# Layer 0's down projection as seven block products of 256 token columns, with its weight sums made earlier in the program

## The chip, the cores and the metric

One core of a Trainium2 chip runs the whole program in one launch. The metric is the device time of one execution in microseconds (us). Instructions go to five engines that run side by side, each strictly in its own order: TensorE (PE in the profile, its weight loads PEld), VectorE (DVE), ScalarE (ACT), GpSimd (POOL) and SyncE (SP). Transfers (DMA) are issued by SP, ACT or POOL and land later.

## The reference

Two layers of a decoder over 512 tokens, width 1024, feed-forward width 2816, all in float32:

```python
for l in range(DEPTH):                                     # DEPTH = 2
    p = rmsnorm(x, norm1_g[l]) @ w_in[l]
    p_rw, p_ret, p_sg, gate_logits = jnp.split(p, in_cuts, axis=-1)
    branches = jnp.stack([rwkv7_branch(p_rw, ...), retention_branch(p_ret, cos, sin),
                          sgu_branch(p_sg, ...)], axis=2)
    proj = jnp.einsum('bsgc,gcd->bsgd', branches, w_branch[l])
    gates = jax.nn.sigmoid(gate_logits.reshape(B, S, N_BRANCH, D_MODEL))
    x = x + jnp.sum(gates * proj, axis=2) @ w_out[l]
    x = x + conv_ffn(rmsnorm(x, norm2_g[l]), ffn_w_up[l], ffn_conv_w[l], ffn_conv_b[l], ffn_w_down[l])
return rmsnorm(x, final_g)
# conv_ffn: u = h @ w_up; causal depthwise convolution of width 3; (silu(gate) * val) @ w_down
```

## The kernel before

Activations lie with features on the 128 partitions and the 512 tokens in the free dimension. A float32 product is made of three matmuls (`mm3`): each operand is split into a high part (a cast, on ScalarE) and a low part (the rest, a subtraction on VectorE), and low x high, high x high and high x low are added in one accumulator. A weight unit is a 128x512 block (256 KB): `load` asks for it on SP's queue, `part` makes its high part (`sh` or `wh`, line 140) and low part (`sl` or `wl`, line 141), and `unit` keeps loads and splits a few units ahead of the matmuls (AHEAD). `acc` and `sm` are accumulators in PSUM.

A layer runs: the input projection with the recurrence (`rwkv`; eight chunks, whose steps on TensorE alternate with `fill`ed matmuls of other projections), then in `mixer` the branch outputs. There the string SEQ orders the pieces: S is a pair of retention chunks, Y (`ret_out`) normalises and transposes the retention output, and 0, 1 and 2 are the merges, the projections of the three branches times their gates. Around Y, VectorE makes `vt` (the gated retention rows, line 999) from `rrr`, a reciprocal root that GpSimd computes (line 996); TensorE transposes `vt` (line 1006); and each merge's accumulator is multiplied by its gate `gth` (line 1074), which was saved to memory (`gd`) earlier and is loaded back on GpSimd's queue (line 1071), then added by GpSimd (line 1077) or VectorE. After the mixer come the output projection (`wout`), the up projection (`ffn_up`, 22 chunks of gate and value columns, with the convolution and the activation `fth`) and the down projection.

Layer 0's down projection (`ffn_down`) takes 8 blocks of 128 output features; each adds 22 chunks of 128 inner features, three 512-column matmuls for each chunk: 528 matmuls. Layer 1's (`last`) is a seven-product block multiplication (Strassen's, in Winograd's form): the token half and the output half are split in two, sums of activations are the left operands (`halves` makes them in `ffn_up`), sums of weights the right ones. The weight sums are made beforehand by `presum`: per q (11 of them, 256 inner features each) four 128x512 loads `pre`<-`wdt` on GpSimd's queue, four VectorE passes (lines 251 to 254) and four stores `ts`; at the place where it is called next, the sums of the loads asked for at the call before are made. PRE says at which call the loads of q are asked for: during layer 0's up projection ("f") and after each output block of layer 0's down projection ("d").

A scheduler orders what the code hands it; instructions marked `kept` or `keep_in_program_order` stay where the code has them.

Of the kernel before, what the change touches and what calls it, by code (L numbers as in the profile page):

```python
# [26 lines left out]
PRE = {(0, "f", 2): 0, (0, "f", 4): 1, (0, "f", 6): 2, (0, "f", 8): 3, (0, "d", 0): 4, (0, "d", 1): 5, (0, "d", 2): 6, (0, "d", 3): 7,  # L27
       (0, "d", 4): 8, (0, "d", 5): 9, (0, "d", 6): 10}
SEQ = "0 H G G 0 S 0 U U G G 0 S 0 0 S 2 2 Y 0 0 2 1 2 1 2 1 2 1 2 1 2 1 1 1"
# [23 lines left out]
class Emit:  # L53
# [68 lines left out]
    def load(self, u, queue=None):  # L122
        name, l, i, c0, n, _ = u
        raw = self.u(n="wr") if u[5] in ("q", "u") and self.nraw % 2 else self.wp.tile([128, 512], F32, name=self.nm("wr"), tag="wr", bufs=NRAW)
        src = self.tsum[i] if name == "tsum" else self.a[name][l, i]
# [4 lines left out]

    def part(self, u):
        raw, n, pool = self.raws.pop(0), u[4], u[5]

# [112 lines left out]
    def presum(self, l, stage, m):  # L246

        if self.pre:
            q, b = self.pre.pop()
            V = self.nc.vector  # L250
            V.tensor_tensor(b[3], b[3], b[1], op=SUB)
            V.tensor_tensor(b[1], b[1], b[0], op=SUB)
            V.tensor_tensor(b[0], b[0], b[3], op=ADD)
            V.tensor_tensor(b[2], b[2], b[0], op=SUB)
            for p, t in zip((7, 5, 6, 4), (b[3], b[1], b[0], b[2])):
                self.tsum[q, p] = self.dp.tile([128, 512], F32, name=self.nm("ts"))
                self.nc.gpsimd.dma_start(self.tsum[q, p], t)
        q = PRE.get((l, stage, m))
        if q is not None:
            b = self.fpre.pop(0) if stage == "f" else [self.u(n="pre") for _ in range(4)]  # L260
            for i, t in enumerate(b):
                self.nc.gpsimd.dma_start(t, self.a["wdt"][0, 2 * q + i // 2][:, i % 2 * 512:i % 2 * 512 + 512])
            self.pre.append((q, b))

# [84 lines left out]
    def run(self):  # L349
        nc, tc, a, V = self.nc, self.tc, self.a, self.nc.vector  # L350
        self.con = self.cp.tile([128, NCC], F32, name="con")
        self.pre, self.tsum = [], {}
# [39 lines left out]
        for l in range(L):  # L392
# [7 lines left out]
            else:  # L400
                st = self.norm_new()
                x, xd = self.ffn_down(l, act, x, st)
# [8 lines left out]
    def mixer(self, l, nst):  # L411
# [27 lines left out]
        rows = iter([((), (0, 1), (0, 1, 2)), ((0, 1), (2, 3)), ((2, 3),)])  # L439
        for step in SEQ.split():  # L440
            if step == "S":
# [52 lines left out]
    def rwkv(self, l, nst):  # L494
# [210 lines left out]
        for c in range(8):  # L705
# [13 lines left out]
            V.tensor_copy(xb, Q[:, 1])  # L719
            self.fill(FILL[2], True)  # L720
# [18 lines left out]
            if c < 7:  # L739
# [3 lines left out]
                else:  # L743
                    V.tensor_tensor(St, St, Q[:, 0], op=ADD)
                    po(V.tensor_tensor(St, St, f, op=MUL))
            py = P1[:, 0]
# [735 lines left out]
```

## Time and profile before

| | |
|---|---|
| median of 3 runs | 1691.85 us (1691.11 to 1692.03) |
| span of the profiled execution | 1688.8 us (3.05 us below that median: what lies around the span) |
| granted TensorE clock | full in all 40 slices |
| busy: PE, DVE, ACT, POOL | 99%, 72%, 47%, 15% |
| layer 0: the merges behind the last retention matmuls, and the output projection | 398.9 to 505.5 |
| layer 0: up projection, down projection | 506 to 733.6, 733.6 to about 853 |
| layer 1: the same merges | from 1242.9 |

Times within a run count from the span's start. A row of the timeline is: start, duration, engine, line, operation, output<-input, shapes, count, and in brackets the idle time before it with what released it. The chain of waits follows the work that ended last backwards; its rows are start, duration, what. A row of the windows is: stretch, its length, busy time and count of the engine asked for (in the first such row below PE, in the later ones DVE), granted clock, share and rate of the DMA queues.

### The profile page before, as it was taken

Reading aid. Unit: us, or ns where it says so; the run is one execution under the profiler, and the core shown is the slowest. Engines: PE = TensorE matmul, PEld = TensorE weight load, DVE = VectorE, ACT = ScalarE, POOL = GpSimd, SP = SyncE. Lnnn points to the kernel's source line nnn. Section 1 sums busy time; section 2 is a strip of 40 time slices with the busy share of each in tenths; the row PEclk is TensorE's granted clock in tenths of the full one; section 3 lists DMA queues with packets and bytes.
Section 4 is the critical chain, followed back from the end, with each engine's and each line's share of the span. In section 5 each row is a group of like instructions: output and inputs, shape, how many; then the busy total and the mean of one; then the engine's idle time right before and its main releaser. Section 6 shows DMA issues by size and latency. Waiting matters only on the chain.

```text
span 1688.8 us, 27952 instructions
## 1 busy us (share of the span) xinstructions
PE 1680.2 (99%) x10247; PEld 1381.5 (82%) x10247; DVE 1217.9 (72%) x2115; ACT 793.7 (47%) x1365; POOL 261.3 (15%) x376
## 2 busy tenths in 40 slices
PE   9999999999999999999999999999999999999998
PEld 7888877888888888888888888778888888888887
DVE  7887746578669877655568888465786688887877
ACT  6563433554255444433346544335542544444565
POOL 1121000312301200003321210003122012220000
PEclk9999999999999999999999999999999999999999
DMA  5236563634544533247743366536344434443775
GB/s 183 88 109 199 176 187 95 184 122 134 191 144 148 195 122 97 63 146 261 252 145 99 94 207 184 174 101 188 118 137 163 154 96 144 142 141 110 244 248 177
DMA packets 143385, 260.01 MB, mean 154 GB/s; under 512 B 19440, under 2 KB 35440, under 8 KB 143248
## 3 DMA queue, kind: packets, MB, share of 16 engines
q1 hardware_dynamic: 117056, 188.41, 35.9%
q0 software_dynamic: 17552, 54.15, 9.8%
q10 hardware_dynamic: 8640, 15.67, 2.6%
q8 instruction: 80, 1.31, 0.3%
q14 instruction: 57, 0.47, 0.1%
HBM read 212.94 MB, written 45.22 MB: 153 GB/s over the span
## 4 chain that ended last, share of the span: by engine, by line
PE 97%; DVE 1%; DMA 1%; issue 0%; ACT 0%; SPq 0%; ACTq 0%; DVEq 0%
PE acc L157 88%; PE sm L157 3%; PE sm L696 2%; PE sm L948 1%; PE sm L603 1%; PE sm L1059 0%; DMA wr<-wall 0%; DMA tr<-bkT 0%; DVE wl L141 0%; PE acc L359 0%; PE sm L566 0%; PE sm L565 0%; PE sm L1006 0%; PE sm L850 0%; PE acc L319 0%
## 5 line engine op out<-in xcount | busy, mean ns | idle before, releaser
L157 PE MATMUL acc<-lo,sh 128*128 128x512 f32 x1108 | 432.0, 390 | 0.0
L157 PE MATMUL acc<-hi,sh 128*128 128x512 f32 x1108 | 431.4, 389 | 0.0
L157 PE MATMUL acc<-hi,sl 128*128 128x512 f32 x1108 | 424.6, 389 | 0.0
L140 ACT CAST sh<-wr 128x512 fp32r<-128x512 f32 (+1 forms) x375 | 226.8, 614 | 309.1 <-PE acc L157 165.6
L141 DVE TENSOR_TENSOR sl<-wr,sh 128x512 fp32r<-128x512 f32 (+1 forms) x375 | 252.0, 680 | 94.9 <-ACT sh L140 78.9
L141 DVE TENSOR_TENSOR wl<-wr,wh 128x512 fp32r<-128x512 f32 x238 | 169.0, 713 | 139.4 <-ACT wh L140 133.6
L140 ACT CAST wh<-wr 128x512 fp32r<-128x512 f32 x238 | 146.8, 619 | 242.8 <-PE acc L157 154.6
L157 PEld LDWEIGHTS acc<-lo,sh 128*128 128x128 f32 x1108 | 208.0, 188 | 43.8 <-issue 0.3
L157 PEld LDWEIGHTS acc<-hi,sl 128*128 128x128 f32 x1108 | 208.0, 188 | 43.1 <-issue 0.2
L157 PEld LDWEIGHTS acc<-hi,sh 128*128 128x128 f32 x1108 | 208.0, 188 | 43.0
L157 PE MATMUL acc<-lo,wh 128*128 128x512 f32 x584 | 230.0, 394 | 0.4 <-DVE rwp L525 0.4
L157 PE MATMUL acc<-hi,wl 128*128 128x512 f32 x584 | 228.3, 391 | 0.1
L157 PE MATMUL acc<-hi,wh 128*128 128x512 f32 x584 | 227.6, 390 | 0.0
L1125 ACT ACTIVATE cv<-fu,pc 128x512 f32<-128x512 f32 x88 | 71.7, 816 | 138.4 <-DVE fu L1123 138.4
L157 PEld LDWEIGHTS acc<-hi,wl 128*128 128x128 f32 x584 | 109.6, 188 | 24.6 <-issue 0.9
L157 PEld LDWEIGHTS acc<-lo,wh 128*128 128x128 f32 x584 | 109.6, 188 | 24.2 <-DVE rwp L525 0.8
L157 PEld LDWEIGHTS acc<-hi,wh 128*128 128x128 f32 x584 | 109.7, 188 | 22.3 <-issue 0.2
L157 PE MATMUL acc<-ah,sh 128*128 128x512 f32 x352 | 108.4, 389 | 0.0
L1126 DVE SCALAR_TENSOR_TENSOR cv<-fu,pc,cv 128x511 f32<-128x511 f32 x88 | 65.8, 749 | 34.5 <-ACT cv L1125 34.4
L157 PE MATMUL acc<-wl,hi 128*128 128x512 f32 x212 | 85.7, 404 | 0.0
L1123 DVE TENSOR_TENSOR fu<-acc,rsF 128x512 f32<-128x512 f32 x88 | 60.3, 685 | 30.8 <-PE acc L157 29.8
L157 PE MATMUL acc<-wh,hi 128*128 128x512 f32 x212 | 82.5, 389 | 0.0
(368 smaller groups left out, 2447.5 us busy)
## 6 DMA issues: line engine op xcount, KB each, us to landing
wr<-wall SPq DMA_DIRECT2D x480, 256.0 KB, 2.9
gd<-gth ACTq DMA_DIRECT2D x48, 256.0 KB, 3.4
gth<-gd POOLq DMA_DIRECT2D x48, 256.0 KB, 3.7
pre<-wdt POOLq DMA_DIRECT2D x44, 256.0 KB, 6.1
ts<-pre POOLq DMA_DIRECT2D x44, 256.0 KB, 2.8
wr<-ts SPq DMA_DIRECT2D x44, 256.0 KB, 4.1
wr<-wdn SPq DMA_DIRECT2D x40, 256.0 KB, 4.3
wr<-wdt SPq DMA_DIRECT2D x33, 256.0 KB, 4.1
```

Source lines behind the costliest of these rows:

```text
L140: self.kept(self.nc.scalar.copy(hi[:, :n], raw[:, :n]))
L141: self.kept(self.nc.vector.tensor_tensor(lo[:, :n], raw[:, :n], hi[:, :n], op=SUB))
L157: i = self.nc.tensor.matmul(*x, **y, **kw)
L603: i = T.matmul(pK[hv[1 - h], j, :], bk[hv[h], c, 1, :], x[hv[h], c, :], start=True, stop=True)
L696: po(T.matmul(o, l, r, start=start, stop=True, skip_group_check=True))
L948: po(T.matmul(o, lhsT, rhs, start=start, stop=stop, skip_group_check=True))
L1123: V.tensor_tensor(u, ps, self.rsF, op=MUL)
L1125: A.activation(t, u, AF.Identity, scale=self.p("cw2", j), bias=self.p("cb", j))
L1126: V.scalar_tensor_tensor(t[:, 1:], u[:, :511], self.p("cw1", j), t[:, 1:], op0=MUL, op1=ADD)
```

## The change

- Layer 0's down projection becomes `down`, the seven-product form with the operands' roles as follows: a weight block 128x128 stays in the array, 256 token columns move. Seven phases (products 1, 6, 2, 7, 5, 4, 3), each 11 units of q, each unit 4 output blocks x 3 matmuls of 128x256: 924 matmuls from 77 weight units (33 straight from `wdt`, 44 from the stored sums `ts`).
- `ffn_up` in layer 0 calls `halves` too; two of the four activation operands of a pair go to memory (`ab`, `s4`) and are read back and split in `down` (`side`).
- The 44 sums for layer 0 are new. Their places and those of layer 1's sums: two at a time in the recurrences (`rsum`, RSUM), at four "P" marks in SEQ among the merges (layer 0: q 3 to 6; layer 1: q 5, 7 and 9), in layer 0's up projection (layer 0's q 7 to 10), and in `down` at units 4 and 10 (layer 1's q 0 and 1), where `presum` is called after each of the first 22 units. For layer 1's q 4, 6 and 8 nothing is stored: the weights are loaded when `last` needs them and summed in place (NOW, `fetch4`, `sum4`).
- The residual and normalisation work of layer 0's end is done on 256-column halves as the products finish; the residual copy `xd` is stored in halves.

The core of the diff:

```diff
+PRE = {(0, "m", 0): (0, 3), (0, "m", 1): (0, 4), (0, "m", 2): (0, 5), (0, "m", 3): (0, 6),
...
+       (0, "d", 4): (1, 0), (0, "d", 10): (1, 1), (1, "m", 0): (1, 5), (1, "m", 1): (1, 7), (1, "m", 2): (1, 9)}
+RSUM = {(0, 0): (0, 0), (0, 2): (0, 1), (0, 4): (0, 2), (1, 0): (1, 2), (1, 2): (1, 3), (1, 4): (1, 10)}
+NOW = ((1, 4), (1, 6), (1, 8))
-SEQ = "0 H G G 0 S 0 U U G G 0 S 0 0 S 2 2 Y 0 0 2 1 2 1 2 1 2 1 2 1 2 1 1 1"
+SEQ = "0 H G G 0 S 0 U U G G 0 S 0 0 S 2 2 Y 0 P 0 2 P 1 2 1 P 2 1 2 P 1 2 1 P 2 1 1 1"
...
+    def sum4(self, b, p):
+        o, i, op = {7: (3, 1, SUB), 5: (1, 0, SUB), 6: (0, 3, ADD), 4: (2, 0, SUB)}[p]
+        return b[o], self.nc.vector.tensor_tensor(b[o], b[o], b[i], op=op)
...
+    def rsum(self, l, c, at):
+        if at and (l, c) in RSUM:
+            t = [self.rw((128, 2, 512), "cs", 3) for _ in range(2)]
+            q, b = RSUM[l, c], [t[i // 2][:, i % 2, :] for i in range(4)]
+            for i in range(4):
+                self.nc.gpsimd.dma_start(b[i], self.raw4(*q, i))
+            self.rs4 = q, b
+        elif (l, c - 2 + at) in RSUM:
+            q, b = self.rs4
+            for p in ((7, 5) if at else (6, 4)):
+                t, i = self.sum4(b, p)
+                self.tc.keep_in_program_order(i)
+                self.keep4(q, p, t)
...
-    def ffn_down(self, l, act, x, st):
-        for m in range(8):
-            ps = self.acc()
-            self.matF(ps, ("wdn", l, m, 0), act)
...
-            self.presum(l, "d", m)
+    def down(self, act, x, st):
...
+        for k, p in enumerate((1, 6, 2, 7, 5, 4, 3)):
...
+            for q in range(Q):
+                n = Q * k + q
+                w = self.unit("tsum", 0, (q, p), 0) if p > 3 else self.unit("wdt", 0, 2 * q + (p > 1), 512 * (p == 3))
+                side(n)
...
+                for j in range(4):
+                    ms, o = slice(128 * j, 128 * j + 128), ps[b][j // 2][:, 256 * (j % 2):256 * (j % 2) + 256]
+                    self.mm3(o, (w[0][:, ms], w[1][:, ms]), (xs[0][:, at:at + 256], xs[1][:, at:at + 256]), ...)
+                post(n)
+                if n < 22:
+                    self.presum(0, "d", n)
```

How the instructions stand after the change, at three places. The first is VectorE around the merges of layer 0. Before, the two `vt` groups of retention chunks 2 and 3 stand between gate passes (`gth`, L1074) and weight splits (`sl`):

```order
L1074 SCALAR_TENSOR_TENSOR gth_891_4552<-gth_891_4552,acc_892_4554 128x512
L994 TENSOR_SCALAR rss_889_4543<-rss_889_4543 128x4
L141 TENSOR_TENSOR sl_932_4707<-wr_920_4659,sh_931_4706 128x512
L999 SCALAR_TENSOR_TENSOR vt_681_3723<-ry_883_4524,rrr_887_4535,vt_681_3723 128x128 x4
L1074 SCALAR_TENSOR_TENSOR gth_896_4575<-gth_896_4575,acc_897_4577 128x512
L141 TENSOR_TENSOR sl_939_4734<-wr_925_4681,sh_938_4733 128x512
L999 SCALAR_TENSOR_TENSOR vt_683_3728<-ry_884_4527,rrr_890_4546,vt_683_3728 128x128 x4
L141 TENSOR_TENSOR sl_944_4757<-wr_930_4704,sh_943_4756 128x512
```

Now the second gate pass is `gth_914`; behind it come, in this order, one split, two sums (L153), a split, three sums, a split and three sums, and then these rows (the last of those sums at the top):

```order
L153 TENSOR_TENSOR pre_956_4777<-pre_956_4777,pre_954_4775 128x512
L169 TENSOR_TENSOR sl_994_4909<-wr_972_4836,sh_993_4908 128x512
L153 TENSOR_TENSOR pre_984_4875<-pre_984_4875,pre_982_4873 128x512
L153 TENSOR_TENSOR pre_982_4873<-pre_982_4873,pre_981_4872 128x512
L1045 SCALAR_TENSOR_TENSOR vt_699_3777<-ry_901_4578,rrr_905_4589,vt_699_3777 128x128 x4
L153 TENSOR_TENSOR pre_981_4872<-pre_981_4872,pre_984_4875 128x512
L1045 SCALAR_TENSOR_TENSOR vt_701_3782<-ry_902_4581,rrr_908_4600,vt_701_3782 128x128 x4
L153 TENSOR_TENSOR pre_983_4874<-pre_983_4874,pre_981_4872 128x512
L178 TENSOR_TENSOR lo_921_4658<-sm_919_4652,hi_920_4657 128x512
```

Eleven sums stand ahead of `vt_701`, the second group. The second place is GpSimd at the same stage. Before, it computes `rrr`, adds two gated merges and loads the next gates:

```order
L996 TENSOR_TENSOR rrr_870_4456<-rss_869_4453,con_78 128x4
L996 TENSOR_TENSOR rrr_887_4535<-rss_886_4532,con_78 128x4
L1077 TENSOR_TENSOR gth_790_4136<-gth_790_4136,gth_891_4552 128x512
L996 TENSOR_TENSOR rrr_890_4546<-rss_889_4543,con_78 128x4
L1077 TENSOR_TENSOR gth_810_4196<-gth_810_4196,gth_896_4575 128x512
L1071 DMA gth_913_4634<-gd_348_1650 128x512
```

Now fourteen `pre` loads stand between `rrr_888` and `rrr_905` (the last two of them are the first rows here), and the next gate load, `gth_931`, stands behind the stores of twelve sums (of which the last four are shown in the second fence):

```order
L284 DMA pre_1006_4965<-wdt 128x512
L284 DMA pre_1007_4966<-wdt 128x512
L1042 TENSOR_TENSOR rrr_905_4589<-rss_904_4586,con_78 128x4
L1042 TENSOR_TENSOR rrr_908_4600<-rss_907_4597,con_78 128x4
L1123 TENSOR_TENSOR gth_808_4190<-gth_808_4190,gth_909_4606 128x512
L1123 TENSOR_TENSOR gth_828_4250<-gth_828_4250,gth_914_4629 128x512
L284 DMA pre_1008_4967<-wdt 128x512
L289 DMA ts_950_4764<-pre_939_4713 128x512
```

```order
L289 DMA ts_1002_4954<-pre_984_4875 128x512
L289 DMA ts_1003_4957<-pre_982_4873 128x512
L289 DMA ts_1004_4960<-pre_981_4872 128x512
L284 DMA pre_1009_4968<-wdt 128x512
L289 DMA ts_1005_4963<-pre_983_4874 128x512
L1117 DMA gth_931_4688<-gd_348_1650 128x512
```

Layer 1 has the same order with twelve loads and ten sums. The third place is VectorE early in layer 0's down projection. Before, the sums of one q stand between the splits of that projection's units, one set per output block (66 matmuls):

```order
L141 TENSOR_TENSOR sl_1639_7745<-wr_1631_7706,sh_1638_7744 128x512
L251 TENSOR_TENSOR pre_1623_7664<-pre_1623_7664,pre_1621_7662 128x512
L252 TENSOR_TENSOR pre_1621_7662<-pre_1621_7662,pre_1620_7661 128x512
L253 TENSOR_TENSOR pre_1620_7661<-pre_1620_7661,pre_1623_7664 128x512
L141 TENSOR_TENSOR sl_1642_7763<-wr_1634_7724,sh_1641_7762 128x512
L254 TENSOR_TENSOR pre_1622_7663<-pre_1622_7663,pre_1620_7661 128x512
L141 TENSOR_TENSOR sl_1658_7806<-wr_1637_7742,sh_1657_7805 128x512
```

Now `sl_1717` and `sl_1724` are the splits of units 8 and 9, the four sums follow at once, and `wl_1731` is the split of unit 10; five units later the same happens ahead of unit 16's split:

```order
L169 TENSOR_TENSOR sl_1717_7908<-wr_1677_7773,sh_1716_7907 128x512
L169 TENSOR_TENSOR sl_1724_7934<-wr_1703_7833,sh_1723_7933 128x512
L153 TENSOR_TENSOR pre_1721_7926<-pre_1721_7926,pre_1719_7924 128x512
L153 TENSOR_TENSOR pre_1719_7924<-pre_1719_7924,pre_1718_7923 128x512
L153 TENSOR_TENSOR pre_1718_7923<-pre_1718_7923,pre_1721_7926 128x512
L153 TENSOR_TENSOR pre_1720_7925<-pre_1720_7925,pre_1718_7923 128x512
L169 TENSOR_TENSOR wl_1731_7964<-wr_1706_7851,wh_1730_7963 128x512
```

The four loads of that set stand on GpSimd directly behind the store of the last pair's `ab`.

More of the change, by code (lines that the diff above doesn't have):

```diff
@@ L249, in presum @@
             q, b = self.pre.pop()
[L250 to L257, printed above, removed]
+            for p in (7, 5, 6, 4):
+                self.keep4(q, p, self.sum4(b, p)[0])
         q = PRE.get((l, stage, m))
@@ L439, in mixer @@
         rows = iter([((), (0, 1), (0, 1, 2)), ((0, 1), (2, 3)), ((2, 3),)])
+        ip = iter(range(8))
         for step in SEQ.split():
-            if step == "S":
+            if step == "P":
+                self.presum(l, "m", next(ip))
+            elif step == "S":
                 self.ret_pair(*next(rows))
@@ L1187, in unit @@
             if p > 3:
-                return self.unit("tsum", 0, (q, p), 0)
-            return self.unit("wdt", 0, 2 * q + (p > 1), 512 * (p == 3))
+                return self.unit("tnow" if (1, q) in NOW else "tsum", 1, (q, p), 0)
+            return self.unit("wdt", 1, 2 * q + (p > 1), 512 * (p == 3))
         def prod(ps, x, at, r, w, first, end, **kw):
```

188 lines of the change are left out of this document (159 added, 29 removed).

## The prediction

> **What bounds the kernel now.** I read the page first (engines, clock, chain of waits), then the windows and the timeline of the stages that the diff touches.
>
> ```profile
> PE 1680.2 (99%) x10247; PEld 1381.5 (82%) x10247; DVE 1217.9 (72%) x2115; ACT 793.7 (47%) x1365; POOL 261.3 (15%) x376
> PEclk9999999999999999999999999999999999999999
> PE 97%; DVE 1%; DMA 1%; issue 0%; ACT 0%; SPq 0%; ACTq 0%; DVEq 0%
> 733.00:852.00 119.00, 119.00 (x527) 1.00 0.71 235
> ```
>
> TensorE is busy 99% at full clock and is 97% of the chain; layer 0's down projection (733 to 852) has no gap. So every matmul removed is time gained, and every wait newly put in front of TensorE is time lost. No cover is needed for what never makes it wait; vector work has 28% of the span free, but only where its order allows.
>
> **The gain: fewer matmul columns.** The chain's long unbroken piece prices a 512-column matmul, the kernel's last 36 accumulations a 256-column one (first and last row):
>
> ```profile
> 412.09 93.42 PE acc L157 x412
> 1678.60 0.28 PE L157 MATMUL acc<-sl,hi 128*128 128x256 f32 x1
> 1682.80 0.28 PE L157 MATMUL sm<-sh,lo 128*128 128x256 f32 x1
> ```
>
> 93.42/412 = 0.2268 us; 4.20/35 = 0.120 us, each with its own weight load. Before: 8 outputs x 22 chunks x 3 = 528 matmuls, 119.7 us. After: 7 x 11 x 4 x 3 = 924, 110.9 us. Gain 8.8 us. [...]
>
> **First loss: the sums at down's start.** `presum` is now called once per weight unit (12 matmuls x 0.120 = 1.44 us) instead of once per output column block (about 15 us). Loads asked for at unit 4 are summed at the next call, and on the vector engine those four sums stand ahead of the low half (`wl`) of unit 10. E is the moment the last up-projection matmul has issued, 733.38 + 0.23 = 733.6. Rows of the chain that leads to the loads, from layer 0 and from layer 1's same code, and then two rounds of presum:
>
> ```profile
> 733.38 0.39 PE L157 MATMUL acc<-hi,sl 128*128 128x512 f32 x1
> 737.09 0.69 DVE L1132 SCALAR_TENSOR_TENSOR fth<-fth,cv 128x512 f32<-128x512 f32 x1
> 1580.98 0.68 DVE L1132 SCALAR_TENSOR_TENSOR fth<-fth,cv 128x512 f32<-128x512 f32 x1
> 1581.77 0.43 DVE L1153 TENSOR_TENSOR wh<-fth,fth 128x256 f32<-128x256 f32 x1
> 1582.69 0.43 DVE L1155 TENSOR_TENSOR wl<-fth,wh 128x256 f32<-128x256 f32 x1
> 1583.03 1.28 DVE L141 TENSOR_TENSOR wl<-wr,wh 128x512 fp32r<-128x512 f32 x2
> 751.05 2.13 POOL L262 DMA_DIRECT2D pre<-wdt  x4
> 759.78 0.69 DVE L251 TENSOR_TENSOR pre<-pre,pre 128x512 f32<-128x512 f32 x1 [2.79 <-DMA pre<-wdt]
> 760.50 0.69 DVE L252 TENSOR_TENSOR pre<-pre,pre 128x512 f32<-128x512 f32 x1
> 763.42 0.54 POOL L257 DMA_DIRECT2D ts<-pre  x1 [0.66 <-DVE pre L254]
> 765.76 2.13 POOL L262 DMA_DIRECT2D pre<-wdt  x4
> 774.89 0.69 DVE L251 TENSOR_TENSOR pre<-pre,pre 128x512 f32<-128x512 f32 x1 [2.61 <-DMA pre<-wdt]
> gth<-gd POOLq DMA_DIRECT2D x48, 256.0 KB, 3.7
> ```
>
> The vector engine waits for these loads today (2.79 and 2.61 us), 8.7 and 9.1 us after the first issue; a unit of 2.7 us hides it. In the new order: the last gated activation starts at E+3.5; +0.8 to the half sums, +0.3 for the extra 256-column subtraction, +0.9, +0.3, two splits 1.2, the last half subtraction 0.4: E+7.5. Only then does GpSimd's store of `ab` issue (0.54), and behind it the four loads, from E+8.1. At 8.7 us the sums start at E+16.8, take 3 x 0.72 + 0.69 = 2.85, and unit 10's split 0.68: E+20.3. TensorE wants it at 10 x 1.44 + 0.24 = E+14.6. Stall 5.7 us. The second set (unit 10) is issued behind the first set's stores, E+20.5 (last sum + 0.84, the 763.42 row), so sums start at E+29.2 and unit 16's split is ready at E+32.7; TensorE, going on at E+20.3, is there after six units, E+28.9. Stall 3.8 us. Together 9.5.
>
> Bounds: if the last load lands 3.7 us after its issue (the gth row), first sum at E+13.9: 2.8 and 0.9, 3.7 in all; if it takes 12 us, because weights now come every 1.44 us instead of 2.72, 9 and 6, 15. I stay at 8.7, the same loads in the same stage. [...]
>
> **Second loss: the merges, both layers.** Rows of layer 0, then layer 1's, which are the same 844.0 us later:
>
> ```profile
> 398.92 5.67 PE acc L157 x24
> 404.58 0.22 PE sm L1006 x2
> 405.41 0.68 DVE L1074 SCALAR_TENSOR_TENSOR gth<-gth,acc 128x512 f32<-128x512 f32 x1
> 403.33 2.16 DVE L999 SCALAR_TENSOR_TENSOR vt<-ry,rrr,vt 128x128 f32<-128x128 f32 x4
> 406.61 2.17 DVE L999 SCALAR_TENSOR_TENSOR vt<-ry,rrr,vt 128x128 f32<-128x128 f32 x4
> 1239.68 1.13 DVE L999 SCALAR_TENSOR_TENSOR vt<-ry,rrr,vt 128x128 f32<-128x128 f32 x4
> 393.52 2.07 POOL L996 TENSOR_TENSOR rrr<-rss,con 128x4 f32<-128x4 f32 x2 [25.74 <-DVE rss L994]
> 403.27 1.28 POOL L1077 TENSOR_TENSOR gth<-gth,gth 128x512 f32<-128x512 f32 x1
> 407.79 2.19 POOL L1071 DMA_DIRECT2D gth<-gd  x4
> 410.67 1.42 PE sm L1006 x13
> 1242.91 5.67 PE acc L157 x24
> 1248.58 0.22 PE sm L1006 x2
> ```
>
> Today both `vt` groups are done at 408.8, before TensorE's transposes at 410.5, so nothing waits. In the new order eleven weight sums (ten in layer 1) and three weight splits stand with them ahead of the second `vt` group. The accumulator pass ahead of it can start when its 24 matmuls are done, about 404.8; then 0.6, one split 0.6, so the sums start at 406.0. Eleven sums at 0.60 (the x2 row: 1.28 - 0.68) to 0.72, say 0.66: 7.3; splits 1.8; two `vt` groups 2 x 1.05; and 1.03 twice, because a group beside GpSimd's addition takes 2.16 instead of 1.13 and two such additions move in here: done at 419.2. TensorE has 36 matmuls behind its first two transposes: 404.80 + 8.16 = 413.0. Stall 6.2 us. Then its next merge needs the fresh split: +0.5 (one cast, one subtraction, nothing else queued). The merge behind that needs an accumulator that is freed by a pass over `gth_931` (the name in the numbered order), whose load GpSimd issues only behind the stores of the twelve sums, about 420.5 instead of 407.8; it lands at 424.2, pass 0.7 us, 424.9; TensorE is there at 419.2 + 1.5 + 0.5 + 12 x 0.227 = 423.9, and a sum whose load is issued still later stands ahead of that pass: 2 us. Layer 0: 8.7; layer 1 with one sum less 8.0.
>
> Bounds, each layer: all loads in time, sums at 0.60, no stretch: stall 3.5, in all 4. Loads at the down stage's pace (four per 8.7 us; GpSimd asks for them from 395.6): the eleventh lands around 420, stall about 12, in all 14.5. I take 8.7: twelve loads and six of weights from 395.6 to 411 are 4.7 MB in 15.4 us, 306 GB/s, what a round of presum moves today:
>
> ```profile
> 766.00:775.00 9.00, 3.14 (x6) 1.00 0.90 300
> 600.00:643.60 43.60, 32.57 (x49) 1.00 0.31 99
> ```
>
> **Third loss: recurrences.** Two sums behind the state update and two behind the XB copy of chunks 1 to 6.
>
> ```profile
> 278.32 0.42 DVE L745 TENSOR_TENSOR S<-S,F 128x256 f32<-128x256 f32 x1
> 278.66 0.17 DVE s L756
> 281.00 0.42 DVE L719 COPY XB<-sm 128x256 f32<-128x256 f32 x1
> 282.57 1.09 PE sm L696 x64
> 283.25 0.69 DVE L141 TENSOR_TENSOR wl<-wr,wh 128x512 fp32r<-128x512 f32 x1 [1.04 <-ACT wh L140]
> ```
>
> At chunks 5 and 6 rotary work already fills the engine: XB is done 1.15 us before TensorE uses it, and two sums are 1.2 to 1.4 us; the next state update loses perhaps 0.9 more. Earlier chunks have idle time. 1.2 us a layer (0 to 1.5): 2.4.
>
> **Costed at nothing.** Layer 0's up projection: a pair of chunks (96 matmuls, 21.8 us) now takes six 256-column passes and one split where two splits stood, 6 x 0.43 + 0.68 - 1.36 = 1.9 more on 16.3 (half the last row's 32.57), and its sums stood there before: 18.2 of 21.8 covered; if that fails, 1 us. Down's 77 units at 0.6 us of splitting per 1.44 us; layer 1's sums in place likewise; its 24 saved transfers save nothing, since no wait stands there. The last phase's tail (about 5 us of vector work) is behind 36 column matmuls (8.2 us).
>
> **Sum.** -8.8 + 9.5 + 8.7 + 8.0 + 2.4 = +19.8 us. The profiled span is 1688.8, 3.05 below the median of 1691.85; the median moves by the same: 1711.7.
>
> **Rivals.**
> (a) Loads land quickly (3.7 us after issue, sums at 0.60): down loses 3.7, merges 4.5 and 4, recurrences 1.2: -8.8 + 13.4 = +4.6, 1696. For it: GpSimd's other loads do that. Against: the same loads' own 8.7 us.
> (b) Loads share the queues with the denser weights: down 15, merges 14 each, 2.4: +36.6, 1728. For it: eight or more loads at once, which the kernel before never has.
> (c) Faster: the cover holds in the merges. If the stretch from the `gth` pass to the second `vt` group takes under 8.2 us instead of 14.4 the vector engine keeps ahead of TensorE's 36 matmuls; then only down's stalls at their low bound stay, -8.8 + 3.7 + 1.2 = -3.9, 1688. It decides below 8.8 us of losses in all. Against: by the shortest rows that stretch is 11.7 us (pass and split 1.2, sums 6.6, splits 1.8, `vt` 2.1).
> (d) The block products give less than counted, e.g. because 77 units of weights at 182 GB/s plus operands reloaded from memory hold TensorE: the window above moves 235 GB/s, the round of presum 300. Part of (b).
>
> **Chances.** Forecast 0.62, (a) 0.18, (b) with (d) 0.13, (c) 0.04, and 0.03 that it lands within 0.2% (3.4 us, about what can be told from no change). Faster 0.04, same 0.04, slower 0.92. The range runs from (a) to just below (b): 1697 to 1727.
>
> **What would show it.** Around 405 to 425 and 844 + that: a gap of TensorE before the transposes, released by `vt`, and vector rows of `pre` in a block ahead of `vt`; a second gap released by a `gth` pass. Around 14 and 29 us after down's start gaps released by `wl`, with a vector wait on the `pre` loads before them. Down's matmuls at 0.120. Wrong if the merges show no gap, or if the `pre` loads are there before the vector engine asks.

## The result: 44 us slower, where 20 were forecast

The changed kernel takes 1735.96 us (median of 4 runs, 1733.88 to 1736.85), the kernel before beside it 1691.49: ratio 1.0261, 95% interval 1.0246 to 1.0275. The direction was right; the time lies 9 us above the range. The matmuls saved in layer 0's down projection gave what was forecast; the new weight sums, and the waits and slower clock that came with them, cost far more. The profiled execution of after has a span of 1732.2 us. Its page (engines, chain) and the cores' row:

```profile
PE 1687.8 (97%) x10643; PEld 1402.3 (81%) x10643; DVE 1297.4 (75%) x2287; ACT 819.3 (47%) x1436; POOL 311.4 (18%) x470
PE 74%; issue 12%; DVE 6%; DMA 4%; POOL 2%; ACT 1%; ACTq 0%; DVEq 0%; SPq 0%; POOLq 0%
core 0: 1732.2 us, clock 0.991
```

TensorE is 74% of the chain, 97% before: in some places the chain of waits now runs through transfers and vector work. And the clock is 0.991: it was full in every slice before. What TensorE waited for (total us, times, longest):

```profile
PE sm L1052 <- DVE vt L1045: 11.4, 4, 5.0
PE acc L185 <- DVE wl L169: 8.4, 5, 4.3
PE acc L185 <- DVE gth L1120: 5.7, 2, 3.9
PE sm L740 <- DVE S L790: 2.8, 4, 1.2
PE sm L740 <- DVE XB L763: 2.1, 1, 2.1
```

The first three are the waits that the prediction named: `vt` and a `gth` pass in the merges, `wl` in down. The next two are the recurrences; the last one is the first step of layer 1's. The table cuts both traces at the same marks of TensorE (first matmul of a stage to the first of the next; in the kernel before, 17 matmuls of 0.227 us that stand ahead of the up projection are counted to it, as in after). The mark at layer 1's recurrence stands behind the gap in its first step, so the row before it holds that gap. The last three columns belong to experiments 9, 10 and 17 below.

| stage, us | before | after | difference | form alone | form, early loads | cheapest places |
|---|---|---|---|---|---|---|
| layer 0, to the end of the recurrence | 289.1 | 290.7 | +1.7 | 289.3 | 289.1 | 292.8 |
| merges and output projection 0 | 97.1 | 111.2 | +14.1 | 97.8 | 97.4 | 98.1 |
| up projection 0 | 231.7 | 231.7 | 0 | 231.7 | 231.7 | 234.2 |
| down projection 0 | 119.7 | 122.0 | +2.3 | 111.0 | 110.9 | 116.5 |
| layer 1, norm to recurrence | 205.8 | 213.3 | +7.5 | 211.3 | 207.6 | 206.6 |
| recurrence 1 | 67.8 | 69.2 | +1.4 | 70.2 | 68.9 | 73.6 |
| merges and output projection 1 | 101.6 | 111.9 | +10.3 | 101.6 | 101.6 | 101.6 |
| up projection 1 and last phase | 332.8 | 337.9 | +5.1 | 333.9 | 334.3 | 334.7 |

The differences make 42.4 of the 43.4 us between the spans.

**The merges.** The chain through layer 0's merges (start, us, what):

```profile
399.57 6.24 DMA pre<-wdt
...
407.43 6.69 DMA pre<-wdt
...
414.15 0.68 DVE pre L153
...
421.06 1.05 DVE vt L1045 x4
...
423.01 0.53 POOL ts L289
423.54 4.43 DMA gth<-gd
...
430.51 0.69 DVE gth L1120
...
DMA to landing us min/median/max: 6.4/6.4/6.5
```

Two loads of `pre` in a row, a block of sums, `vt`; then the store of a sum, the gate load queued behind it, its pass. The last row is the answer for the four gate loads issued from 423.5 to 425.5: they took 6.4 us to land, so the first was there at 429.9, and not at 427.97, where its row of the chain ends. Three sums (428.45 to 430.6) stood ahead of its pass as well. TensorE's gaps, start to start: 5.41 and 1.65 us before `vt`'s transposes, 0.57, and 4.25 before the matmul behind that gate pass; in layer 1 3.57, 2.38, 0.58 and 2.19. Less the ordinary spacing they make 11.1 and 7.9 us. In layer 1 the last gap has another cause: the first gate load had landed at 1296.3, but its pass (1297.7) stood behind a weight split that waited for TensorE's own matmuls.

**Down.** The chain, then the first wait's row, then rows behind it:

```profile
757.83 0.52 POOL pre L284
...
770.37 7.87 DMA pre<-wdt
...
778.26 0.70 DVE pre L153
...
781.05 0.69 DVE wl L169
768.60 0.39 PE L185 MATMUL acc<-ah,wl 128*128 128x256 f32 x1 [4.32 <-DVE wl L169]
...
770.02 0.42 PE L185 MATMUL acc<-ah,wl 128*128 128x256 f32 x1
770.24 0.63 PE L185 MATMUL acc<-ah,wh 128*128 128x256 f32 x2
770.66 0.41 PE L185 MATMUL acc<-ah,wl 128*128 128x256 f32 x1
...
823.62 15.84 PE sm L185 x132
```

Once the sums are through, a matmul takes what was costed: 15.84/132 = 0.120 us (last row). The gaps are 764.00 to 768.60 and 778.71 to 781.79. But behind the first gap, from 770.02 to 770.66, three matmuls take 0.64 us instead of 0.36.

**The clock.** Windows of after (stretch, length, TensorE busy and count, granted clock, DMA share, GB/s): the six stretches at half clock in which TensorE has work, then one behind a gap of 2.34 us in layer 1's recurrence, at full clock; below, the merges of layer 0 before and after (each engine's busy time, then the clock):

```profile
418.00:424.80 6.80, 3.90 (x16) 0.51 1.02 382
431.70:435.10 3.40, 3.40 (x10) 0.52 0.57 219
769.60:773.00 3.40, 3.40 (x18) 0.52 0.88 240
783.20:786.60 3.40, 3.40 (x18) 0.51 0.96 302
906.10:909.50 3.40, 3.40 (x10) 0.51 0.43 151
1288.40:1295.20 6.80, 5.54 (x20) 0.51 0.83 295
...
1084.90:1088.30 3.40, 3.40 (x72) 1.00 0.72 223
```

```profile
395.00:440.00 45.00, 45.00 (x226) 37.60 (x225) 33.22 (x58) 15.86 (x29) 16.38 (x20) 1.00 0.49 158
395.00:440.00 45.00, 34.94 (x164) 28.55 (x163) 35.18 (x65) 11.76 (x22) 29.33 (x45) 0.89 0.79 281
```

Each stretch is 3.41 us or twice that and lies behind a gap of 3.1 us or more, or behind a cluster of gaps (902 to 906). TensorE is busy in 23.0 of their 27.2 us, so they cost at most 11.5. In down it is 3.0 (16 matmuls in each of two stretches, at 0.213 instead of 0.120 us); what the gaps leave over of the merges' loss is 3.0 of 14.1 and 2.4 of 10.3; with 1.6 at layer 1's start that is about 10 us of TensorE's time. It is not what a full clock would have saved: no run changed the clock alone, and where the next wait ends with a load, as behind the first stretch in down, a faster TensorE would only have waited longer.

The length of a gap alone does not decide: the longest of that cluster is 1.64 us, the one that full clock follows 2.34. In after's record of the granted clock the changes between full and half all lie on one grid of 3.413 us (the stretches between them last 3.413, 6.827, 10.24 us and so on), and half clock went with how long TensorE had worked within the window of that grid ahead. The window of after ahead of the stretch at 906; then, of experiment 12, one with a gap of 2.40 us and the half clock behind it; last, of experiment 7, the first of two windows that share a gap of 3.35 us, with no half clock behind either:

```profile
902.58:905.99 3.41, 1.59 (x7) 1.00 0.21 77
881.93:885.34 3.41, 1.40 (x7) 1.00 0.23 77
885.34:888.75 3.41, 3.41 (x10) 0.50 0.60 210
1116.91:1120.32 3.41, 1.79 (x8) 1.00 1.00 277
```

After's trace has 496 full-clock windows on that grid. All six in which TensorE was busy for less than 45% (0.24 to 1.32 us) were followed by half clock; of three between 46 and 49% one was (that at 902.58), and of the 487 above 58% none.

### The profile page after: what moved, and what is told of

Read it like the earlier page. It is cut to its first block, busy times and chain, and to the rows that moved or that the text cites. A ratio compares the mean times of both kernels' runs of the same rounds, so it can differ in the third digit from the quotient of the medians.

```text
span 1732.2 us, 29278 instructions
## 1 busy us (share of the span) xinstructions
PE 1687.8 (97%) x10643; PEld 1402.3 (81%) x10643; DVE 1297.4 (75%) x2287; ACT 819.3 (47%) x1436; POOL 311.4 (18%) x470
## 4 chain that ended last, share of the span: by engine, by line
PE 74%; issue 12%; DVE 6%; DMA 4%; POOL 2%; ACT 1%; ACTq 0%; DVEq 0%; SPq 0%; POOLq 0%
PE acc L185 66%; PE sm L185 4%; PE sm L740 2%; DMA pre<-wdt 2%; DVE wl L169 1%; DVE sl L169 1%; DVE pre L153 1%; PE sm L647 1%; DMA wr<-wall 1%; PE sm L994 0%; ACT wh L168 0%; PE sm L1105 0%; DMA wr<-ts 0%; POOL pre L284 0%; POOL ts L289 0%
## 5 line engine op out<-in xcount | busy, mean ns | idle before, releaser
L185 PE MATMUL acc<-lo,sh 128*128 128x512 f32 (+1 forms) x1144 | 444.9, 389 | 6.2 <-DVE gth L1120 5.7
L185 PE MATMUL acc<-hi,sh 128*128 128x512 f32 (+1 forms) x1144 | 443.8, 388 | 0.0
L185 PE MATMUL acc<-hi,sl 128*128 128x512 f32 (+1 forms) x1144 | 431.1, 388 | 0.0
L168 ACT CAST sh<-wr 128x512 fp32r<-128x512 f32 x352 | 212.0, 615 | 183.6 <-PE acc L185 83.7
L169 DVE TENSOR_TENSOR wl<-wr,wh 128x512 fp32r<-128x512 f32 x278 | 194.7, 706 | 136.0 <-ACT wh L168 131.8
L169 DVE TENSOR_TENSOR sl<-wr,sh 128x512 fp32r<-128x512 f32 x352 | 239.0, 692 | 68.7 <-ACT sh L168 60.2
L185 PE MATMUL acc<-lo,wh 128*128 128x512 f32 (+1 forms) x636 | 245.0, 385 | 0.0
L185 PE MATMUL acc<-hi,wl 128*128 128x512 f32 (+1 forms) x636 | 243.3, 382 | 0.8 <-DVE wl L169 0.8
L185 PE MATMUL acc<-hi,wh 128*128 128x512 f32 (+1 forms) x636 | 242.5, 381 | 0.0
L185 PEld LDWEIGHTS acc<-hi,wl 128*128 128x128 f32 x636 | 119.7, 188 | 25.4 <-DVE wl L169 1.8
L185 PEld LDWEIGHTS acc<-lo,wh 128*128 128x128 f32 x636 | 119.7, 188 | 23.8 <-DVE rwp L569 0.4
L185 PEld LDWEIGHTS acc<-hi,wh 128*128 128x128 f32 x636 | 119.7, 188 | 22.1 <-issue 0.2
L185 PE MATMUL acc<-wh,lo 128*128 128x512 f32 x212 | 82.5, 389 | 0.0
```

The costliest lines, as they stand in the source:

```text
L168: self.kept(self.nc.scalar.copy(hi[:, :n], raw[:, :n]))
L169: self.kept(self.nc.vector.tensor_tensor(lo[:, :n], raw[:, :n], hi[:, :n], op=SUB))
L185: i = self.nc.tensor.matmul(*x, **y, **kw)
```

## The experiments

The ratios are to the kernel before, run beside each (1690.3 to 1691.4 us); stage times are from each run's trace. Layer numbers in the edits count from 0.

**1. Down's sums spaced out.** `presum` is called at three units only:

```diff
-                if n < 22:
+                if n in (4, 10, 16):
```

> The changed kernel with the weight sums in layer 0's down projection asked for at units 4 and 10 and summed at units 10 and 16 instead of 5 and 11. Theory (sums whose loads have not landed hold up the splits behind them): both gaps of TensorE in that stage (4.6 and 3.1 us) go, and with them the two stretches of half clock behind them (about 3.3 us): 10 to 11 us less than the changed kernel, about 1725. Rival (the stage is short of transfer bandwidth with 77 weight units): the gaps move to a later unit and the time stays within 3 us.

1723.1 us, ratio 1.019 (1.0161 to 1.022). Down falls from 122.0 to 111.8 us; `wl`'s waits:

```profile
PE acc L185 <- DVE wl L169: 1.8, 3, 1.0
```

Both gaps and their half-clock stretches are gone: the same eight sums cost 0.9 us when six units instead of one lie between loads and sums. Their order, not their number, made down's loss.

**2. Layer 0's merges cleared.** Its four sets go to the up projection:

```diff
-PRE = {(0, "m", 0): (0, 3), (0, "m", 1): (0, 4), (0, "m", 2): (0, 5), (0, "m", 3): (0, 6),
+       (0, "f", 10): (0, 3), (0, "f", 12): (0, 4), (0, "f", 14): (0, 5), (0, "f", 16): (0, 6),
```

> The changed kernel with layer 0's four sets of weight sums taken out of its merges and made in layer 0's up projection (chunks 10 to 16) instead. Theory (the sums among the merges cost 14 us in that layer, the up projection covers them): about 14 us less, 1722, and no gap of TensorE around 405 to 435. Rival (the vector engine is too full in the up projection, or what is late in the merges is not the sums): gaps appear between 600 and 700, or the gap before the transposes stays; less than 5 us gained.

1726.2 us, 1.0209 (1.0179 to 1.0238). The stage returns to 97.1 us (-14.1), the up projection pays 1.2. So this price is the merges' own. The time falls by 10 only, since other stages of that execution were longer.

**3. No vector passes in the merges,** loads and stores kept (`keep4` gets the loaded tile):

> The changed kernel with the vector passes of the weight sums left out in the merges of both layers; their loads and stores stay as they are (the stores write unsummed weights, so the result is another one). Theory (eleven and ten vector passes stand ahead of the second vt group): the gaps before the transposes (5.4 + 1.7 and 3.6 + 2.4 us) mostly go; the later gap by a gate pass (4.3 and 2.2) may stay, since its load is still behind the stores; 10 to 16 us less in all. Rival (GpSimd's queue is the cause: fourteen loads stand ahead of the reciprocal roots): the gaps before the transposes stay above 3 us; at most 6 us less.

1732.3 us, 1.0245 (1.0187 to 1.0302). `vt`'s gaps shrink from 5.41 and 1.65 to 2.15 and 1.05, but the gate gap grows from 4.25 to 7.14: the stages gain 1.7 and 2.2 us only. The chain there:

```profile
414.82 1.60 POOL ts L289 x3
416.42 5.39 DMA ts<-pre
...
423.66 5.75 DMA gth<-gd
...
429.44 0.70 DVE gth L1120
```

GpSimd's stores and loads, in order, take the place of the vector engine.

**4. The gate loads on SP's queue** (`nc.sync.dma_start` at line 1117):

> The changed kernel with the gate loads of the merges asked for on SP's queue instead of GpSimd's, where they stand behind the weight sums' loads and stores. Theory A (in the merges two things are late one behind the other: the vector block ahead of vt, and the gate load behind the stores): the gaps before the transposes stay (about 5 to 7 us in layer 0, 5 to 6 in layer 1), the gaps released by a gate pass (4.3 and 2.2) go; 6 to 10 us less with the half clock behind them. Theory B (it is the transfers' landing, whatever queue): the gate gaps stay within 1 us of what they were.

1745.0 us, 1.0319 (1.0299 to 1.034). The gate gaps vanish and others come (2.42, 0.81 and 3.17 us later in layer 0's merges); the stage grows to 117.3. This is no way round the queue.

**5. The loads alone in the merges,** passes and stores left out:

```diff
+            if stage != "m" and q in ((0, 3), (0, 4), (0, 5), (0, 6), (1, 5), (1, 7), (1, 9)):
+                return
...
-                self.keep4(q, p, self.sum4(b, p)[0])
+                if stage != "m":
+                    self.keep4(q, p, self.sum4(b, p)[0])
```

> The changed kernel with vector passes and stores of the weight sums left out in the merges of both layers, their loads kept (unsummed weights are used in their place, so the result is another one). Theory (in the merges GpSimd's queue is the second limit: the gate load stands behind stores that wait for the loads): with the stores gone the gate gaps (7.1 and 3.6 us without the passes) shrink below 2 us, the stages lose 8 us or more each against the changed kernel. Rival (the loads alone fill the transfer queues): the gate gaps stay above 4 and 2 us.

1715.5 us, 1.0149 (1.0128 to 1.0169). The merges lose 3.3 and 3.0 us instead of 14.1 and 10.3, without gate gaps. So three limits stand one behind the other: passes ahead of `vt`, stores ahead of the gates, and some 3 us of the loads.

**6. No passes in the last phase's in-place sums:**

> The changed kernel with the in-place weight sums of layer 1's down projection left out (the unsummed weights are split and used instead). Theory (twelve passes more on a vector engine whose splits TensorE waits for there): the six gaps of 0.7 to 0.8 us around 1641 to 1705 go and the stage from layer 1's second norm to the end loses 4 to 5 us. Rival (the 24 direct loads, or their buffers, hold it up): under 1.5 us.

1735.0 us, 1.026 (1.024 to 1.0281), no gain, because other stages of that execution were longer; but the stage falls from 337.9 to 333.9, and the gaps of 0.72 to 0.80 us at 1641 to 1666 are gone. About 4 of its 5.1 us are these sums.

**7. No passes in the recurrences,** loads and stores kept:

> The changed kernel with the vector passes of the weight sums left out in both recurrences, loads and stores kept (the stores write unsummed weights). Theory (two passes behind the state update and two behind the XB copy): the gaps of 1.57 us at chunks 5 and 6 of both layers go; 2 to 3 us less. Rival (the loads disturb the transfers that the recurrence itself waits for): the gaps of 1.6 and 2.3 us in its first chunks stay, and so does most of the loss.

1745.2 us, 1.0321 (1.0291 to 1.035). The 1.57-us gap at chunk 6 is gone; new ones (3.51 and 3.35 us the longest) stand where the chain goes through a transfer:

```profile
208.26 4.69 DMA bkS<-tr
...
219.26 1.98 PE sm L738 x62
```

Here the loads can disturb more than the passes; how much varies between executions (1741.1 and 1749.2 us).

**8. The two `wua` loads of layer 1 ahead of both casts:**

> The changed kernel with the two small weight loads at the start of each layer (wua, on ScalarE's queue) both issued ahead of the casts that read them. Theory (at layer 1's start ScalarE stands 2.2 us at a load issued just ahead of its reader, which delays the norm factor and piles up work until TensorE waits at 888 and 903 to 907): the stage from the norm to the recurrence loses 4 to 5 us of its 7.5, about 1731. Rival (the pile-up is from the vector engine's halves at the end of down, or from late weight loads): under 1.5 us.

1738.4 us, 1.028 (1.0251 to 1.031). ScalarE's wait shrinks from 2.18 to 0.41 us, the gap at 888 is gone, one of 2.44 at 906 takes its place. Moved by a few instructions only, the loads gain nothing that shows.

**9. The form alone,** no weight sum in either layer (products use unsummed blocks):

> The seven-product form in both layers with every weight sum left out (no loads, passes or stores for them; unsummed weight blocks of the same size are used where sums stood, so the result is another one). Theory (the form gains 8.8 us by its matmuls and all the loss is the sums' and their places'): down takes 111 to 112 us against 119.7, the merges and recurrences are as before, 1683 to 1686. Rival (the form costs by itself at layer 1's start, where its tail of halves comes late): the stage behind layer 1's first norm stays 3 to 5 us longer than before, 1687 to 1690.

1688.3 us, 0.9993 (0.9983 to 1.0002). Down gives its full 8.7, the merges are as before, and yet the time is the same: layer 1's start costs 5.5 us and its recurrence 2.4 in the profiled execution, which took 3.7 us more than the median of its ten runs. The chain there:

```profile
850.67 3.56 DMA wua<-wua
854.26 2.69 DMA wua<-wua
...
858.90 0.70 ACT rms L332
```

The norm's factor (`rms`) comes behind two `wua` loads, which ScalarE issues only once the tail's halves are through it.

**10. The same, with these loads issued at unit 66 of down:**

```diff
+                if n == 66:
+                    self.wua1 = [self.u(n="wua") for _ in range(2)]
+                    for i in range(2):
+                        self.tc.keep_in_program_order(nc.scalar.dma_start(self.wua1[i], self.a["wua"][1, i]))
```

> The kernel with the new products and none of the weight sums (as the earlier run that leaves them all out and makes its split operands from unsummed tiles), with one more edit: layer 1's two loads of wua are issued at unit 66 of the first down projection instead of right ahead of their casts. Theory (the late wua load is what the new form itself pays at the start of layer 1, because ScalarE issues it only behind the tail's halves and then waits 2.2 us for it): the stretch from layer 1's norm to its recurrence falls from 211.2 us to 208 to 209, the products of down stay at 111, and the time is 1685 to 1686, 0.25 to 0.35% below the kernel before. Rival (the pile-up some 22 us behind the norm, where TensorE waits for split operands of the late wall tile, is set by other loads): the stretch stays at 210.5 to 211.5 and the time at 1688 to 1689.

1684.6 us, 0.9961 (0.9947 to 0.9974): layer 1's start falls by 3.6 to 207.6, the recurrence by 1.3 (the profiled execution is 2.0 us above its median). By the medians of 9 and 10 the late loads cost 3.7 us, the larger part of what the form itself costs; with them early it is worth 6.2 us. What is left for 22 sets of sums (11 of them made before as well) is thus 0.28 us a set.

**11. The sums spread over both up projections** (20 of 22 sets), and **12.** fewer there, three sets in each recurrence (both with the loads of experiment 8):

> The changed kernel with its weight sums put elsewhere: layer 0's q 0 to 9 in layer 0's up projection (chunks 2 to 20), layer 1's q 1 to 9 in layer 1's up projection, one of layer 1's in down (asked for at unit 4, summed at unit 14), one of each layer in the recurrence (asked for at chunk 2); none among the merges, none in place; and both small loads at a layer's start ahead of their casts. Theory (the block products' gain of 8.8 us is there, and all the loss came from where the sums stand): 1683 to 1690, so up to 8 us faster than before, with 3 to 5 us kept by layer 1's start. Rival (the seven-product form costs by itself, through 77 weight units and the reloaded operands): no faster than before.

> The changed kernel with its weight sums where the runs so far found each set cheapest: layer 0's in its up projection (chunks 2 to 16, eight sets) and recurrence (three), layer 1's in down (asked for at units 4 and 14, summed at 14 and 24), in its recurrence (three) and up projection (six). From the stages of the earlier runs: 1.2 + 2 + 1 + 3 + 6 us of losses and 2 to 4 at layer 1's start against 8.8 gained: 1696 to 1701, still no faster than before. Rival (the losses per set shrink when they stand apart): 1688 or less.

1704.1 us, 1.0079 (1.0062 to 1.0096), and 1698.7, 1.0052 (1.0036 to 1.0068). In 11 the up projections pay 4.6 and, with the last phase, 9.1 us; in 12 0.2 (layer 0, eight sets) and 4.0, but the first recurrence 4.9. In the merges at most 0.9 us is left.

**13 and 14. Sums on GpSimd, and the same places on VectorE:**

```diff
-        return b[o], self.nc.vector.tensor_tensor(b[o], b[o], b[i], op=op)
+        return b[o], self.nc.gpsimd.tensor_tensor(b[o], b[o], b[i], op=op)
```

> All 88 weight sums are made, on GpSimd (128x512 additions of 1.28 us there in the trace of before) instead of VectorE, at other places: layer 0's q 0 to 9 loaded in its up projection (one set for each pair of chunks), q 10 and layer 1's q 0 to 7 in down (at units 4, 10, 17, ... 59), layer 1's q 8 to 10 in its own up projection; none in the merges, the recurrences or in place; the two wua loads of layer 1 are issued at unit 66 of down. Theory (a sum costs time because it stands in VectorE's queue ahead of splits and passes that TensorE waits for): on GpSimd the sums cost next to nothing, so the time is that of the form without any sums and with the early wua load, 1684.6, plus 1 to 5 us for TensorE's waits on late weight operands: 1686 to 1690; layer 0's up projection 231.7 to 233, down 111 to 113. Rival (transfers, 88 loads and 88 stores of 256 KB, are what disturbs, or GpSimd's additions slow the vector engine): 1693 to 1702, layer 0's up projection 235 or more and down 113 or more as with VectorE's sums.

> The same places for all 88 sums and the same early wua loads, with the sums on VectorE. Theory: 0.7 us of the vector engine for each of the 40 sums in layer 0's up projection, where it is 82% busy without them, costs 4 to 5 us there as in an earlier run with ten sets; the 36 sums in down stand ahead of unit splits, 1 to 3 us; layer 1's three sets 2 to 3 us: 1692 to 1696. Rival (only transfers count): the same time as with the sums on GpSimd, within 2 us.

1787.9 us, 1.0591 (1.056 to 1.0623) against 1715.3, 1.0146 (1.013 to 1.0161): both theories fall. On GpSimd layer 0's up projection grows by 34 us. Rows of VectorE, then of GpSimd, from one place of it; then one of each from layer 1's up projection:

```profile
558.18 1.74 DVE L170 TENSOR_TENSOR sl<-wr,sh 128x512 fp32r<-128x512 f32 x1 [0.88 <-ACT sh L169]
559.85 1.99 DVE L1207 TENSOR_TENSOR ah<-fth,ah 128x256 fp32r<-128x256 f32 x1
558.09 1.29 POOL L154 TENSOR_TENSOR pre<-pre,pre 128x512 f32<-128x512 f32 x1 [5.42 <-DMA pre<-wdt]
560.24 1.30 POOL L154 TENSOR_TENSOR pre<-pre,pre 128x512 f32<-128x512 f32 x1
...
1508.87 0.68 DVE L1174 TENSOR_TENSOR fu<-acc,rsF 128x512 f32<-128x512 f32 x1
1509.01 1.28 POOL L154 TENSOR_TENSOR pre<-pre,pre 128x512 f32<-128x512 f32 x1
```

A split that takes 0.68 us elsewhere takes 1.74 beside a GpSimd addition, a 256-column subtraction 1.99 instead of 0.42; both end 0.3 to 0.5 us behind the addition. The pass that reads an accumulator (last two rows) stays at 0.68 with an addition beside it. Over the stage (506 to 733) the split's mean is 0.915 us against 0.684 in 14, the subtraction's 0.678 against 0.419, the accumulator pass's 0.681 against 0.683. So GpSimd's additions held up these two passes, whose operands are both tiles, and not the one that reads an accumulator; by what means was not shown. On VectorE nine sets in down cost 24.6 us, three in layer 1's up projection nothing.

**15 and 16. Eight sets in the output projections, or between recurrence and merges** (the rest in the up projections, two in down):

> All 88 sums on VectorE, none of them in the merges, the recurrences, in place, and only two sets in down: layer 0's q 0 to 3 and layer 1's q 2 to 5 are loaded in the output projections (one set for each second output block, 48 matmuls or 10.9 us, where the vector engine is 36 to 66% busy in most stretches of the form without sums), layer 0's q 4 to 10 in its up projection (f 2 to 14), layer 1's q 0 and 1 in down (units 4 and 14), q 6 to 10 in its up projection (every second pair). The two wua loads early, as before. Theory (a sum costs only where the vector engine has no slack until TensorE needs something of it): the time of the form without sums and with the early loads, 1684.6, plus 0.2 to 0.7 in the up projection, 0.7 in down and 0 to 2 in the output projections: 1686 to 1689, 0.1 to 0.3% below the kernel before. Rival (88 loads and stores cost by themselves about 0.1 us each, wherever they stand): 1692 to 1700.

> As the run with eight sets in the output projections, but those eight sets (layer 0's q 0 to 3, layer 1's q 2 to 5) are loaded and summed in the stretch between a layer's recurrence and its merges (from some 300 to 365 us, and the same place of layer 1), where the vector engine is 44 to 67% busy in most of the ten-us stretches and GpSimd waits; everything else is unchanged. The loads use tiles of the feed-forward pool, since the other pool is full there. Theory (a sum costs only where the vector engine, or the queue behind it, has no slack before TensorE needs something of it): the output projections go back to 97.1 and 101.6 us, the stretch between recurrence and merges stays at 113.8 or grows by at most 1 us a layer, the rest stays: the profiled span is 1684 to 1687, the time 1685 to 1688, 0.15 to 0.3% below the kernel before. Rival (sums cost wherever they stand): the stretch grows by 3 us a layer or more, 1691 to 1700.

1707.9 us, 1.0098 (1.0081 to 1.0115), and 1707.7, 1.0095 (1.0079 to 1.0112). In 15 nearly all the loss lies in the output projections (5.7 and 15.6 us). Windows of VectorE in layer 0's (busy, clock, DMA share, GB/s), and the end of layer 1's chain:

```profile
475.00:485.00 10.00, 7.71 (x14) 1.00 1.01 358
485.00:495.00 10.00, 10.00 (x17) 1.00 0.98 378
...
1340.54 6.72 DMA xi<-xd
...
1351.06 6.33 DMA xi<-xd
...
1358.25 3.75 PE acc L187 x8
```

In layer 0 the transfers are full (a share of 0.98 to 1.01) at 358 to 378 GB/s; in layer 1 the residuals `xi` land too late. Their tiles come from the ring that the sums' loads also use; whether that or the full queues delay them was not separated. In 16 the output projections are back at 97.1 and 101.6, and the stretches from recurrence to merges grow by 10.0 and 12.0, in splits and activations that stand behind sums and late loads. An idle vector engine was not free room.

**17. All 88 sums at the cheapest places seen** (up projections 13 sets, down 3, recurrences 6; `wua` early):

> All 88 sums on VectorE, each at the cheapest place that the runs so far showed: layer 0's q 0 to 7 in its up projection, q 8 to 10 in its recurrence; layer 1's q 0 to 2 in down (units 4, 14, 24), q 3 to 7 in its up projection (every second pair), q 8 to 10 in its recurrence; the wua loads of layer 1 early. Theory (the price of a set is that of its place): the form without sums with the early loads, 1684.6, plus 0.2 in the up projection, 1 in down, 1 in the last two stages, 2 to 5 in the first recurrence and 1 in the second: 1689 to 1693, that is within 0.2% of the kernel before. Rival (every set costs about 1 us or more, wherever it stands): 1697 or more.

1701.5 us, 1.0057 (1.0044 to 1.0071): nearer to the rival. In the profiled execution (1.8 us above the median) a third set in down costs some 5 us, three in each recurrence 3.7 and 4.7. Over experiment 10 this is 16.8 us for 22 sets, 0.76 each, against the 0.28 that would break even. No kernel with all its sums that ran here beats the kernel before.

## Why the prediction was right or wrong

- **Right: the gain.** 0.120 us a matmul, 110.9 us without sums: -8.8 as worked out.
- **Right: the mechanism in down.** The first wait ended 19.6 us after the last up-projection matmul (forecast 20.3), the second 32.8 (32.7); the waits were 4.6 and 3.1 (forecast 5.7 and 3.8). How close the ends came is partly luck: the four loads landed 7.2 and 9.5 us after the first issue, where 8.7 was taken for both. The second wait's length is too: the half clock brought TensorE to it some 1.5 us late, so at full clock it would have been about 4.6 by this estimate. The working lacked the half clock; gaps and clock are 10.4 of the 11.1 us that the stage loses against 110.9. Experiment 1 undoes all but 0.9 of it.
- **Wrong, the step that failed first: "Costed at nothing".** Two rows of the table that were put at zero hold 12.6 us, half of what the forecast missed. The in-place sums of the last phase were dismissed with the up projection's cover, without a row of that phase; they cost 4 of its 5.1 us. Layer 1's start was covered by "the last phase's tail is behind 36 column matmuls": the tail's vector work was, but ScalarE's `wua` loads, which stand behind the tail's halves in its order, were not looked at. That is 3.6 of the form's own 5.5 us in the profiled executions (experiments 9 and 10); the other 1.9 stay open. What after's row has beyond these 5.5 is the gap of 2.34 us in the recurrence's first step.
- **Right in place, mis-sized: the merges.** `vt`, then in layer 0 the gate pass behind the stores, as forecast. The term "Layer 0: 8.7; layer 1 8.0" measured 14.1 and 10.3. In layer 1 the gaps alone are 7.9; the clock adds 2.4. In layer 0 the gate term (2 us forecast) was 4.25, `vt` with 6.7 close to the 6.2, and the clock adds 3.0. The gate term was taken at one landing of 3.7 us behind its issue; the load took 6.4, beside full queues (337 to 382 GB/s from 418 to 431.7, a share of 0.96 to 1.02).
- **The recurrences:** right in layer 0 (1.7, forecast 1.2). In layer 1 the table's 1.4 leave out the gap of the first step; with it they are 3.7. The chain there goes through two transfers (`tr` 4.57 and `bkS` 3.73 us). Experiment 1, with the same sums there, has no such gap, so it is no fixed price of them.
- **Wrong: one clock for all terms.** Every term took full speed. Stalls of 3 to 6 us were forecast in four places; that TensorE is slower behind them, about 10 us of its time in all, was not. How much of that a full clock would have saved stays open.
- Of the 24.7 us between the 19.8 forecast and the 44.5 measured, the merges are 7.7, layer 1's start with the gap behind it 7.5, the last phase 5.1, down 1.6 and the recurrences 0.7; some 2 lie outside the table's stages.
- Rival (b), loads that share the queues, came nearest by its number (1728). Its 14 us fit layer 0's merges, and there the queues were full; but the loads alone cost 3.3 and 3.0 us (experiment 5), so they are a part of the cause at most, and down lost 11.1 us against its 15. Rival (a) is out by its size, rival (c) because TensorE waited in both merges.

## What to carry to other kernels

Price a sum by what stands behind it in each in-order queue it uses (its load and store too), by the tiles it holds and by the transfers of that stretch, not by the engine's idle share: the same set cost nearly nothing in one stage and 3 us in the next. Where stalls of the size met here are forecast (2.40 us sufficed in experiment 12), look at what the clock does behind them. And for every reordered tail, list what each queue issues next: two small loads behind new ScalarE work cost some 4 us of a clean 8.7-us gain.

## What the runs showed of the hardware

- In after the clock halved for 3.41 us or twice that at a time (matmuls at 0.213 instead of 0.120 us), on a grid of 3.413 us, behind a window in which TensorE was busy for less than about half: six of six windows under 45%, one of three between 46 and 49%, none of 487 above 58%. A gap of 2.40 us sufficed (12); one of 3.35 us over two windows did not (7).
- Beside GpSimd's additions two VectorE passes over two tiles took longer (13): 0.42 us became 1.99, 0.68 became 1.74; a pass that reads an accumulator did not change (0.68).
- Taking away the work that ends a wait moved it to the next queue three times: from VectorE's passes to GpSimd's stores (3), from the gate load to later ones (4), from sums to transfers (7).
